# A decoder layer on one core: the first weight sums wait for the input's fetches, differences in place, five prepared weights moved into the mixer

## The chip, the cores and the metric

The kernel runs on one core of a Trainium2 chip. The time is device microseconds (us) of one execution; a kernel's time is the median of its runs. TensorE (PE) multiplies matrices, VectorE (DVE) and ScalarE (ACT) do element-wise work, GpSimd (POOL) does some of that and also issues transfers, and SyncE (SP) only issues transfers. Each engine takes its instructions in the order in which they stand in its own queue and waits at an instruction whose operands are not there.

## The reference

One layer: a SwiGLU feed-forward added at half weight, a mixer (stick-breaking attention beside a Mamba-2 scan), cross-attention on 256 memory tokens, and a second SwiGLU feed-forward, each between two RMS norms. The two feed-forwards are what the change touches most.

```python
D_MODEL, SEQ, D_FF = 1024, 1024, 2816

def swiglu(h, w_gu, w_down):
    gu = h @ w_gu
    g, u = jnp.split(gu, 2, axis=-1)
    return (jax.nn.silu(g) * u) @ w_down

    h = h + 0.5 * rmsnorm(swiglu(rmsnorm(h, ffn1_pre_g), ffn1_w_gu, ffn1_w_down), ffn1_post_g)
    h = h + rmsnorm(hybrid_mixer(rmsnorm(h, mix_pre_g), w_in, ...), mix_post_g)
    h = h + rmsnorm(memory_cross_attention(rmsnorm(h, xa_pre_g), rmsnorm(mem, mem_g), ...), xa_post_g)
    h = h + 0.5 * rmsnorm(swiglu(rmsnorm(h, ffn2_pre_g), ffn2_w_gu, ffn2_w_down), ffn2_post_g)
```

## The kernel before

**Every product in three.** An operand is split into a high part of fewer bits (cast on ScalarE) and the rest (subtracted on VectorE); `mm3` multiplies high by high, high by low and low by high. A weight tile of 128 x 1024 numbers or an input tile therefore costs a cast and a subtraction before TensorE can use it (`split`, lines 274 and 276).

**Seven products instead of eight.** The input stands transposed, as 8 tiles of 128 features for each of two halves of 512 tokens. Seen as a 2 x 2 matrix of blocks (B11 and B12: features 0 to 3 of half 0 and 1; B21 and B22: features 4 to 7), and gate and up weights as a 2 x 2 matrix too (G0, G1, U0, U1: their feature halves), a gate and an up column block need seven products of sums and differences. On the weights' side these sums are made on GpSimd for every block pair `f` (`pieces`: five of the seven blocks are sums, into a buffer `wc`, and then split). On the input's side they are made once for each feed-forward: S1 = B11 + B22, S4 = B11 + B12, S5 = B21 + B22, and in place B21 - B11 and B12 - B22, for `k` = 0 to 3. `seven(f)` runs the seven products: B22 and B21 into banks `a` and `b`, S1 into `c`, S4 into a fourth, and then B12 on top of `a`, S5 on top of `c` and B11 on top of `b`. Between them ScalarE copies `a` and `b` (lines 817 and 821), GpSimd takes their difference `d` (line 822), and VectorE makes `e = d + c` (line 827); the product with S5 may not write `c` before that `e` has read it. The first 3 block pairs of feed-forward 1 and the first 4 of feed-forward 2 are done plainly, with 24 matmuls for each gate or up block and half, while the sums are made.

**How the input's sums come about in feed-forward 1.** GpSimd issues the fetches: `fetch(k)` gets the four tiles of B11, B22, B12 and B21 for `k` (into `raw2`, two buffers, and `blk`), ("ca", k) gets B21 and B11 once more, and `again(k)` fetches B12 and B22 into the same buffers (`braw`; `rpost` and `dg`; `acc0` and `acc1`; `cb`). `steps(k)` are S1, S4 and S5, `below(k)` is B21 - B11, `differ(k)` the difference B12 - B22, and `last(k)` splits it. In feed-forward 2, `last(k)` scales B22, makes the difference in a buffer `wc` (three of them, shared with the weights' sums) and splits that.

**What sets the order.** TensorE's order is the program's. `self.clock` counts nominal nanoseconds of TensorE (216 for a matmul of 512 columns); `self.later` holds the side work with the clock from which it is written out, and `at(t, ...)` enters it there. Side work written out of `self.later` keeps the program's order on its engine (`kp`); the rest is placed by a scheduler by its priorities, so that an instruction can come to stand ahead of ones that the program writes earlier. The weights' sums are of the latter kind. `pinned` places the small matmuls of a norm at a clock.

**Prepared weights.** While feed-forward 1 runs, weights of the mixer are split ahead of time and put back to memory as high and low parts (`prepare`): for each half tile a fetch of 256 KB, a cast on ScalarE (line 212), a subtraction on VectorE (line 216) and two stores of 256 KB. `prepare_all` does this for 20 tiles of the scan's projection and the first `QKV` of the 24 tiles of q, k and v, at the clocks in `a`; transfers from clock 418000 on are issued by GpSimd, earlier ones by SyncE. The rest of the 24 are prepared in the scan (`ssd`), with SyncE issuing, which also issues the loads of the scan's own weights.

**Down-projection (`down7`).** Again seven products, over `m`, each of 11 row blocks; for `m` = 1, 2 and 3 TensorE goes on adding to the four banks of `m - 1`, once ScalarE (lines 1083, 1085, 1088) or VectorE has copied what stands there.

Of the kernel before, what the change touches and what calls it, by code (L numbers as in the profile page):

```python
# [14 lines left out]
ALU = mybir.AluOpType  # L15
# [10 lines left out]
MIXED = 6  # L26
QKV = 17
MEM = 256
# [19 lines left out]
class Kern:  # L48
# [200 lines left out]
    def prepare_all(self, sp):  # L249
        names = [("ssd", i) for i in [*range(6), *range(12, 26)]] + [("qkv", i) for i in range(QKV)]  # L250
        pairs = [
            ((self.fp, "acc0", None), (self.fp, "acc1", None)), ((self.fp, "rpost", None), (self.tp, "dg", None)),
            ((sp, "bh", None), (sp, "bl", None)),
        ]
        raw = [(sp, "braw", 2), (sp, "braw", 2), (self.xp, "xl0", KT + 1), (self.xp, "xl1", KT + 1)]
        n = 2 * len(names)
        a = [152000 + 4100 * i for i in range(n)]
        k = sum(t < 416000 for t in a)
        self.prepare(names, raw, pairs, a[:k] + [420000 + 12000 * i for i in range(n - k)], 418000)

# [308 lines left out]
    def up_phase(self, sp, sp2, wgu, gpre, act_d, bank, load, plain, sizes, rw=None, begin=None):  # L569
# [162 lines left out]
        def last(k):  # L732
            b, d = tmp["bd", k]
            if begin:
                self.split(*B12[k], b)
                return
            scale(d, k + 4)
            combine(B12[k], b, k, d, ALU.subtract)

# [12 lines left out]
        def pieces(f):  # L752
# [4 lines left out]
            for a, b, op in (  # L757
# [3 lines left out]
                if b is not None:  # L761
                    t = self.t(sp if begin else sp2, [P, 4, P], F32, "wc", bufs=NWC)
                    nc.gpsimd.tensor_tensor(out=t, in0=a, in1=b, op=op)  # L763
                    a = t
# [95 lines left out]
        Wb = blocks()  # L860
        t0, dt = (T0 + 12000, 7000) if begin else (T0 + 31000, 6500)
        early = [("ad", k) for k in range(4)] if begin else []
# [345 lines left out]
    def ssd(self, close):  # L1208

        nc, ap = self.nc, self.ap  # L1210
        with self.tc.tile_pool(name=self.nm("ssa"), bufs=1, reuse_waits="tile") as ep, \
# [344 lines left out]
            for i, ti in enumerate((8, 10, 0, 1)):  # L1556
                ps = self.proj_now(next(W), 1)
                if i == 0:
                    self.flush(1)
                    self.prepare(  # L1560
                        [("qkv", i) for i in range(QKV, 24)], *self.prep_pool(wsp),
                        [self.clock + 9000 + 8000 * i for i in range(2 * (24 - QKV))],
                    )
# [639 lines left out]
    def run(self):  # L2203
        nc, tc, ap = self.nc, self.tc, self.ap
        with tc.tile_pool(name="const", bufs=1) as cp, tc.tile_pool(name="state", bufs=1, reuse_waits="tile") as xp, \
# [54 lines left out]
            def begin(step):  # L2260
                if step < 0:
                    warm()
                elif step == 0:
                    load_x(0)
                elif step == 1:
                    consts()
                    norm_x(0, 8500, 13500)
                else:
                    load_x(1)
                    norm_x(1, 24000, 28000)  # L2270

# [112 lines left out]
```

## Time and profile before

| | |
|---|---|
| median of 3 runs | 2631.57 us (2626.02 to 2632.20) |
| the profiled execution's own time | 2630.33 us |
| its span, first to last instruction | 2628.6 us |
| TensorE busy | 2584.9 us, 98% of the span, 12850 matmuls |
| VectorE, ScalarE, GpSimd busy | 76%, 49%, 23% |
| memory traffic | 186 GB/s on average, 489.82 MB |

The profile is of one execution of the program. "Busy" is the time in which an engine runs at least one instruction; a matmul is counted as busy from its issue to its modelled end, so that matmuls overlap, and 98% does not mean that TensorE issues at its full rate all the time. A row of a timeline gives the start, the duration, the engine, the line of the kernel, the operation, what is written and read, and in brackets how long the engine was idle before it and what ended the wait. "PEclk" is the share of its full clock that TensorE was granted.

### The profile page before, as it was taken

To read this page: it belongs to the slowest core of one execution; us is meant where nothing else is said; L and a number is where in the kernel's file an instruction comes from. 1 tells how busy PE (TensorE), PEld (TensorE's weight loads), DVE (VectorE), ACT (ScalarE), POOL (GpSimd) and SP (SyncE) were. 2 spreads that over 40 slices of the span, in tenths; PEclk is the share of its full clock that TensorE was granted. 3 is DMA by queue.
4 is the path that set the end of the run, shared out by engine and by line. 5 is a ranking of instruction groups with operands and counts; after the bars stand their busy time and mean duration, and the time that the engine had idled before them with its cause. 6 is when DMAs were issued, how large, how long until landed. Compare 5 with 4: busy or idle time off the path is not lost. (4 is left out here: it accounts for less than half of the span.)

```text
span 2628.6 us, 36857 instructions
## 1 busy us (share of the span) xinstructions
PE 2584.9 (98%) x12850; PEld 2152.0 (82%) x12850; DVE 1988.5 (76%) x3044; ACT 1292.8 (49%) x2300; POOL 595.9 (23%) x708
## 2 busy tenths in 40 slices
PE   9899999999999999999999999999999999999999
PEld 7788888778777778888888897888878788888887
DVE  6878887779679775777777777767556888777767
ACT  7434444545356563555555555345554433333553
POOL 2555553110100001111111110101011655552000
PEclk9999999999999999999999999999999999999999
DMA  6458888875655226655555556547658453326654
GB/s 223 169 187 292 292 282 288 276 253 156 245 183 170 81 73 207 171 144 149 144 155 132 168 158 219 192 149 248 197 191 293 137 178 115 101 96 227 190 171 153
DMA packets 213546, 489.82 MB, mean 186 GB/s; under 512 B 26544, under 2 KB 35120, under 8 KB 213360
## 3 DMA queue, kind: packets, MB, share of 16 engines
q1 hardware_dynamic: 164192, 371.84, 43.8%
q0 software_dynamic: 25840, 73.16, 9.3%
q10 hardware_dynamic: 23328, 42.48, 4.3%
q8 instruction: 101, 1.65, 0.3%
q14 instruction: 85, 0.70, 0.1%
HBM read 327.46 MB, written 138.94 MB: 177 GB/s over the span
## 5 line engine op out<-in xcount | busy, mean ns | idle before, releaser
L139 PE MATMUL mm<-xh,whi 128*128 128x512 f32 x1320 | 520.2, 403 | 3.1 <-ACT xh L281 1.6
L139 PE MATMUL mm<-xl,whi 128*128 128x512 f32 (+1 forms) x1252 | 487.1, 389 | 2.2 <-DVE xl L276 1.7
L139 PE MATMUL mm<-xh,wlo 128*128 128x512 f32 x1272 | 488.5, 391 | 0.0
L139 PEld LDWEIGHTS mm<-xh,whi 128*128 128x128 f32 x1320 | 248.3, 188 | 44.7 <-issue 3.8
L139 PEld LDWEIGHTS mm<-xh,wlo 128*128 128x128 f32 x1272 | 238.8, 188 | 52.1 <-DVE wlo L276 0.4
L139 PEld LDWEIGHTS mm<-xl,whi 128*128 128x128 f32 x1252 | 236.1, 189 | 37.1 <-DVE xl L276 3.3
L1770 DVE TENSOR_TENSOR_SCAN nb<-nb,begin 128x128 f32<-128x128 f32 (+7 forms) x128 | 171.5, 1352 | 51.9 <-ACT nb L1766 51.0
L1766 ACT ACTIVATE nb<-z,scale 128x128 f32<-128x128 f32 (+2 forms) x192 | 107.9, 581 | 77.5 <-PE z L139 77.2
L276 DVE TENSOR_TENSOR wlo<-wraw,whi 128x1024 fp32r<-128x1024 f32 x70 | 85.5, 1221 | 54.1 <-ACT whi L274 50.7
L274 ACT CAST whi<-wraw 128x1024 fp32r<-128x1024 f32 (+1 forms) x87 | 83.8, 965 | 75.1 <-PE mm L139 52.3
L1787 POOL DMA_DIRECT2D mix<-sq x64 | 52.9, 826 | 229.8 <-DVE sq L1785 170.9
L670 ACT ACTIVATE ft<-ft 128x512 f32<-128x512 f32 x88 | 55.5, 632 | 99.2 <-DVE ft L669 98.5
L139 PE MATMUL dn<-xh,wlo 128*128 128x512 f32 x296 | 101.2, 390 | 1.3 <-DMA wlo<-dwlo 1.3
L763 POOL TENSOR_TENSOR wc<-wraw,raw 128x512 f32<-128x512 f32 x56 | 79.8, 1426 | 67.4 <-DVE whi L276 19.8
L763 POOL TENSOR_TENSOR wc<-raw,wraw 128x512 f32<-128x512 f32 x55 | 80.2, 1458 | 52.8 <-DVE wlo L276 21.8
L276 DVE TENSOR_TENSOR atl<-tr,ath 128x512 fp32r<-128x512 f32 (+1 forms) x108 | 67.9, 631 | 29.9 <-ACT ath L274 29.6
L848 POOL TENSOR_TENSOR ft<-ft,e 128x512 f32<-128x512 f32 x37 | 59.7, 1614 | 123.3 <-DVE e L847 47.6
L139 PE MATMUL mm<-ath,v 128*128 128x256 f32 x320 | 85.6, 290 | 0.5 <-ACT sq L1784 0.4
L274 ACT CAST ath<-tr 128x512 fp32r<-128x512 f32 (+1 forms) x108 | 58.9, 546 | 55.0 <-PE tr L142 50.7
L139 PE MATMUL dn<-xh,blk 128*128 128x512 f32 x264 | 85.1, 389 | 0.0
L274 ACT CAST whi<-wc 128x512 fp32r<-128x512 f32 x80 | 49.7, 621 | 68.7 <-PE dn L139 27.4
L139 PE MATMUL mm<-atl,v 128*128 128x256 f32 x320 | 82.7, 281 | 0.7 <-DVE atl L276 0.7
(584 smaller groups left out, 6801.6 us busy)
## 6 DMA issues: line engine op xcount, KB each, us to landing
whi<-dwhi SPq DMA_DIRECT2D x82, 512.0 KB, 3.7
wlo<-dwlo SPq DMA_DIRECT2D x82, 512.0 KB, 4.9
wraw<-in_w_gu SPq DMA_DIRECT2D x43, 512.0 KB, 4.2
raw<-in_w_gu SPq DMA_DIRECT2D x37, 512.0 KB, 4.2
dwhi<-bh SPq DMA_DIRECT2D x67, 256.0 KB, 4.3
dwlo<-bl SPq DMA_DIRECT2D x67, 256.0 KB, 4.3
wraw<-xs SPq DMA_DIRECT2D x56, 256.0 KB, 3.1
xs<-ft ACTq DMA_DIRECT2D x54, 256.0 KB, 3.1
```

The costliest lines, as they stand in the source:

```text
L139: self._pe(self.nc.tensor.matmul(out, lhsT, rhs, start=start, stop=stop, skip_group_check=self.more), cost)
L274: self.kp(self.nc.scalar.copy(hi, src))
L276: self.nc.vector.tensor_tensor(out=lo, in0=src, in1=hi.bitcast(F32), op=ALU.subtract)
L670: nc.scalar.activation(t, t, AF.Silu)
L763: nc.gpsimd.tensor_tensor(out=t, in0=a, in1=b, op=op)
L848: nc.gpsimd.tensor_tensor(out=t1, in0=t1, in1=e, op=ALU.mult)
L1766: nc.scalar.activation(nb[:, s0:s1], z[:, 0:n], AF.Sigmoid, scale=sc[:, i : i + 1])
L1770: nc.vector.tensor_tensor_scan(out=nb[:, 0:Wd][:, ::-1], data0=nb[:, 0:Wd][:, ::-1], data1=begin[:, S - Wd : S][:, ::-1], initial=0.0, op0 ...
L1787: nc.gpsimd.dma_start(out=self.mix_d[p][a * 64 : a * 64 + 64, csl], in_=o, accum_op=ALU.add)
```

## The change

Six edits. The weights' sums of the first block pair that goes through `seven` in feed-forward 1 now keep the program's order on GpSimd. `last` now scales B22 and makes the difference in place (`differ`) in feed-forward 2 too, and splits `b` in both; feed-forward 1 made it in place already, at an earlier clock, and does so still. `QKV` goes from 17 to 12: ten half tiles fewer in feed-forward 1 (64 in place of 74), ten more in the scan (24 in place of 14). The clocks in `a` begin 4000 earlier, stop at 388000 instead of 416000, and go on at 446000 in steps of 9000 instead of 420000 in steps of 12000: 59 and 5 half tiles, where it was 65 and 9. The step between the input's `k` in feed-forward 1 goes from 7000 to 6000, and that between half tiles in the scan from 8000 to 7000. The norm of the input's second half is pinned 2000 and 2500 earlier.

```diff
--- before.py
+++ after.py
@@ -24,7 +24,7 @@
 NFF = 22
 PLAIN = 3, 4
 MIXED = 6
-QKV = 17
+QKV = 12
 MEM = 256
 EPS = 1e-6
 
@@ -254,9 +254,9 @@
         ]
         raw = [(sp, "braw", 2), (sp, "braw", 2), (self.xp, "xl0", KT + 1), (self.xp, "xl1", KT + 1)]
         n = 2 * len(names)
-        a = [152000 + 4100 * i for i in range(n)]
-        k = sum(t < 416000 for t in a)
-        self.prepare(names, raw, pairs, a[:k] + [420000 + 12000 * i for i in range(n - k)], 418000)
+        a = [148000 + 4100 * i for i in range(n)]
+        k = sum(t < 388000 for t in a)
+        self.prepare(names, raw, pairs, a[:k] + [446000 + 9000 * i for i in range(n - k)], 418000)
 
     def wsrc(self, name, i):
         return self.ready[name, i] if (name, i) in self.ready else self.ap["w_" + name][i]
@@ -731,11 +731,10 @@
 
         def last(k):
             b, d = tmp["bd", k]
-            if begin:
-                self.split(*B12[k], b)
-                return
-            scale(d, k + 4)
-            combine(B12[k], b, k, d, ALU.subtract)
+            if not begin:
+                scale(d, k + 4)
+                differ(k)
+            self.split(*B12[k], b)
 
         def differ(k):
             b, d = tmp["bd", k]
@@ -760,7 +759,9 @@
             ):
                 if b is not None:
                     t = self.t(sp if begin else sp2, [P, 4, P], F32, "wc", bufs=NWC)
-                    nc.gpsimd.tensor_tensor(out=t, in0=a, in1=b, op=op)
+                    inst = nc.gpsimd.tensor_tensor(out=t, in0=a, in1=b, op=op)
+                    if begin and f == first_seven:
+                        self.tc.keep_in_program_order(inst)
                     a = t
                 n = self.nblk = (self.nblk + 1) % (6 + NBLK)
                 if n < 6:
@@ -858,7 +859,7 @@
 
         self.nblk = -1
         Wb = blocks()
-        t0, dt = (T0 + 12000, 7000) if begin else (T0 + 31000, 6500)
+        t0, dt = (T0 + 12000, 6000) if begin else (T0 + 31000, 6500)
         early = [("ad", k) for k in range(4)] if begin else []
         homes = {}
         if begin:
@@ -1559,7 +1560,7 @@
                     self.flush(1)
                     self.prepare(
                         [("qkv", i) for i in range(QKV, 24)], *self.prep_pool(wsp),
-                        [self.clock + 9000 + 8000 * i for i in range(2 * (24 - QKV))],
+                        [self.clock + 9000 + 7000 * i for i in range(2 * (24 - QKV))],
                     )
                     close()
                     sp = late.enter_context(self.tc.tile_pool(name=self.nm("ssb"), bufs=1, reuse_waits="tile", side="right"))
@@ -2267,7 +2268,7 @@
                     norm_x(0, 8500, 13500)
                 else:
                     load_x(1)
-                    norm_x(1, 24000, 28000)
+                    norm_x(1, 22000, 25500)
 
             self.kv_d = [[tc.dram_tile([P, 4, MEM], F32R, name=f"kv{h}{n}") for n in range(2)] for h in range(4)]
             self.h = [[ap["xT"][d, :, hh * H : (hh + 1) * H] for d in range(KT)] for hh in range(2)]
```

The order in which instructions stand moves at many places. Three are shown.

GpSimd near the beginning of feed-forward 1, before. Line 763 is the weights' sum and line 686 the input's fetches; `raw2` and `blk` belong to `fetch(k)`, the `braw`, `rpost`, `dg` to ("ca", k):

```order
L763 TENSOR_TENSOR wc_264_864<-wraw_261_854 128x512
L686 DMA raw2_146_542<-in_xT 128x512 x2
L686 DMA blk_147_545<-in_xT 128x512 x2
L686 DMA braw_232_674<-in_xT 128x512
L686 DMA braw_233_675<-in_xT 128x512
L686 DMA rpost_234_678<-in_xT 128x512
L686 DMA dg_235_679<-in_xT 128x512
L686 DMA raw2_236_692<-in_xT 128x512 x2
```

And with the change, further down the queue, where that sum (now line 762) stands:

```order
L686 DMA cb_243_796<-in_xT 128x512
L686 DMA braw_246_816<-in_xT 128x512
L686 DMA braw_247_817<-in_xT 128x512
L686 DMA rpost_249_836<-in_xT 128x512
L686 DMA dg_250_837<-in_xT 128x512
L762 ISA
L762 TENSOR_TENSOR wc_254_854<-wraw_251_844 128x512
```

The first sum moved from ahead of `fetch(2)` to behind the second fetch (`again`) of `k` = 0 and 1, and ("ca", 0) from ahead of `fetch(3)` to behind it.

VectorE in the first block pair of `seven` in feed-forward 1, before. The lines 276 are the low parts of weight blocks (`blk`, `whi`, `wlo` are places of weight tiles) and of B12 - B22 (`xl1`), line 827 is `e`:

```order
L276 TENSOR_TENSOR xl1_31_107<-cb_274_904,xh13_15_91 128x512
L276 TENSOR_TENSOR blk_293_1031<-wc_292_1029,blk_293_1031 128x512
L276 TENSOR_TENSOR blk_296_1051<-wraw_267_871,blk_296_1051 128x512
L276 TENSOR_TENSOR whi_299_1072<-wc_298_1070,whi_299_1072 128x512
L276 TENSOR_TENSOR wlo_302_1093<-wc_301_1091,wlo_302_1093 128x512
L827 TENSOR_TENSOR e_68_184<-sq1_282_962,dn_288_1005 128x512
```

With the change (line 884 multiplies the last plain gate block by its up block, line 742 is `differ`, line 828 is `e`):

```order
L742 SCALAR_TENSOR_TENSOR rpost_249_836<-rpost_249_836,params_3_78,dg_250_837 128x512
L884 TENSOR_TENSOR ft_259_866<-ft_259_866,mm_270_921 128x512
L276 TENSOR_TENSOR whi_255_856<-wc_254_854,whi_255_856 128x512
L276 TENSOR_TENSOR whi_267_913<-wc_266_911,whi_267_913 128x512
L276 TENSOR_TENSOR wlo_269_918<-wc_268_916,wlo_269_918 128x512
L742 SCALAR_TENSOR_TENSOR acc0_261_874<-acc0_261_874,params_3_78,acc1_262_875 128x512
L742 SCALAR_TENSOR_TENSOR cb_264_894<-cb_264_894,params_3_78,cb_265_895 128x512
L276 TENSOR_TENSOR whi_274_954<-wraw_251_844,whi_274_954 128x512
L276 TENSOR_TENSOR wlo_277_973<-wc_276_971,wlo_277_973 128x512
L276 TENSOR_TENSOR xl1_28_104<-braw_246_816,xh10_12_88 128x512
L828 TENSOR_TENSOR e_68_184<-sq1_272_952,dn_278_995 128x512
```

`e` moved from behind all four low parts of B12 - B22 and four of the next block pair to behind the first of the four; the low part of the very first weight block (`whi_255`) now stands behind two differences and behind line 884.

GpSimd in feed-forward 2, before, where the first block pair of `seven` (weights `wraw_4440`, `raw2_4441`) meets the second (`raw2_4465`, `wraw_4466`); line 822 is `d`:

```order
L763 TENSOR_TENSOR wc_4487_20492<-wraw_4440_20194,raw2_4441_20196 128x512
L763 TENSOR_TENSOR wc_4490_20511<-raw2_4441_20196 128x512
L822 TENSOR_TENSOR sq1_4471_20418<-sq1_4471_20418,sq0_4470_20417 128x512
L763 TENSOR_TENSOR wc_4492_20529<-raw2_4465_20381 128x512
L763 TENSOR_TENSOR wc_4499_20573<-raw2_4465_20381,wraw_4466_20383 128x512
```

With the change (line 823 is `d`):

```order
L762 TENSOR_TENSOR wc_4483_20488<-wraw_4440_20194,raw2_4441_20196 128x512
L762 TENSOR_TENSOR wc_4486_20507<-raw2_4441_20196 128x512
L762 TENSOR_TENSOR wc_4488_20525<-raw2_4465_20381 128x512
L762 TENSOR_TENSOR wc_4495_20569<-raw2_4465_20381,wraw_4466_20383 128x512
L762 TENSOR_TENSOR wc_4500_20592<-wraw_4466_20383,raw2_4465_20381 128x512
L762 TENSOR_TENSOR wc_4505_20630<-raw2_4465_20381,wraw_4466_20383 128x512
L823 TENSOR_TENSOR sq1_4471_20418<-sq1_4471_20418,sq0_4470_20417 128x512
```

`d` moved behind four sums of the next block pair.

## Prediction

> **What bounds the kernel now.** I read the page's table of busy time first, then the waits of TensorE alone, then windows of 30 us around the longest of them.
>
> ```profile
> PE 2584.9 (98%) x12850; PEld 2152.0 (82%) x12850; DVE 1988.5 (76%) x3044; ACT 1292.8 (49%) x2300; POOL 595.9 (23%) x708
> ```
>
> TensorE sets the time; the change removes none of its matmuls, so all that can be won is where it waits. The rows give who waits, for whom, the sum, how often, and the longest:
>
> ```profile
> PE dn L139 <- DVE e L827: 5.9, 2, 5.7
> PE mm L139 <- DVE e L827: 3.3, 2, 2.8
> PE dn L139 <- ACT F L1088: 3.1, 1, 3.1
> PE dn L139 <- ACT F L1083: 2.8, 1, 2.8
> PE mm L139 <- DVE xl L276: 1.7, 3, 0.7
> ```
>
> A wait also leaves TensorE slower behind it. These windows show busy time, and behind each "x" the matmuls issued; the last is undisturbed:
>
> ```profile
> 85.00:115.00 30.00, 22.60 (x86) 17.04 (x85) 25.54 (x30) 13.89 (x25) 20.15 (x16) 0.89 0.29 99
> 475.00:505.00 30.00, 27.15 (x114) 22.08 (x113) 22.37 (x37) 17.31 (x33) 3.21 (x6) 0.94 0.78 263
> 540.00:570.00 30.00, 26.86 (x112) 21.75 (x111) 21.16 (x35) 13.74 (x26) 2.15 (x4) 0.94 0.67 220
> 655.00:685.00 30.00, 28.32 (x124) 22.39 (x123) 22.00 (x38) 12.41 (x22) 5.35 (x10) 0.94 0.79 275
> 2085.00:2115.00 30.00, 27.17 (x114) 22.10 (x113) 26.68 (x30) 10.54 (x19) 19.84 (x17) 0.94 0.49 156
> 2125.00:2155.00 30.00, 30.00 (x135) 24.82 (x134) 24.94 (x30) 10.34 (x18) 19.89 (x17) 1.00 0.56 175
> ```
>
> Undisturbed, 135 matmuls go in 30 us. Before the changed places 49, 21, 23 and 21 are missing (first, second, third and fifth row). What one costs stands in the timeline of TensorE:
>
> ```profile
> 85.61 2.88 PE L139 MATMUL dn<-S,whi 128*128 128x512 f32 x12
> 88.33 2.88 PE L139 MATMUL dn<-S,wlo 128*128 128x512 f32 x12
> ...
> 102.37 5.10 PE L139 MATMUL dn<-S,wlo 128*128 128x512 f32 x12 [5.71 <-DVE e L827]
> ```
>
> Twelve start within 88.33 - 85.61 = 2.72 us, 0.227 each; behind the wait the same twelve take 5.10 where 2.88 is usual. So the places cost 11.1, 4.8, 5.2 and 4.8 us: 25.9 in all, 1% of the time, of which the waits are 16.1 (5.7 + 1.7 + 2.8 + 3.1 + 2.8) and the lower clock most of the rest. The Trainium skill (TensorE: Matmul & The Clock Gate, "Why this matters for your kernels") has the clock fall behind gaps over about 3 us; the granted clock of 0.94 around a 2.8 us wait shows a fall at a little less here. By the page the two waits of 2.8 us would be worth their bare length, and the sum below 2 to 4 us less.
>
> **The start of feed-forward 1 (11.1 us).** On GpSimd the first sum holds the queue:
>
> ```profile
> 46.94 1.29 POOL L763 TENSOR_TENSOR wc<-wraw 128x512 f32<-128x512 f32 x1 [30.32 <-DMA wraw<-in_w_gu]
> 50.83 1.09 POOL L686 DMA_DIRECT2D raw<-in_xT  x2 [2.60 <-issue]
> ...
> 59.27 1.06 POOL L686 DMA_DIRECT2D raw<-in_xT  x2 [4.18 <-issue]
> ```
>
> `fetch(2)` goes at 50.83, `fetch(3)` at 59.27, yet the sum alone costs them little: each also waits until VectorE has read the buffer's last user, which these two do:
>
> ```profile
> 49.54 0.74 DVE L702 SCALAR_TENSOR_TENSOR bl<-blk,params,raw 128x512 f32<-128x512 f32 x1
> ...
> 57.98 0.74 DVE L702 SCALAR_TENSOR_TENSOR bh<-blk,params,raw 128x512 f32<-128x512 f32 x1
> ```
>
> Those ends (50.28, 58.72) are what the norm's earlier pins and the shorter step move. The second half's norm comes 2500 of the clock earlier (2.6 us); I let the two reads follow by about 3 us, since on VectorE less stands ahead of them. So the fetches go near 47.5 and 55.5. The first sum and the second fetches come later in the queue than the fetches, and the price is the other end of this edit: the first sum is made not at 46.94 but behind `again(1)`, issued here so far:
>
> ```profile
> 77.24 0.56 POOL L686 DMA_DIRECT2D rpost<-in_xT  x1 [0.86 <-DVE bh L702]
> ...
> 95.28 1.73 POOL L822 TENSOR_TENSOR sq<-sq,sq 128x512 f32<-128x512 f32 x1
> ```
>
> 3 us earlier that is 74.2; two issues of 0.54 and 1.3 for the sum give 76.6. The first of the seven products starts 24 matmuls before 85.61, at 80.2; its third matmul needs the low part of this sum, which on VectorE stands behind the difference `rpost` (its tile lands and is scaled at 83.36 + 0.73 now, so near 80 or 81) and behind the gate times up product, which needs the matmul ending at 80.2. With 0.7 for each of the three and one stretched by a sum on GpSimd (1 more), it is done near 82.5 to 83: TensorE waits about 2.2 us where it did not wait.
>
> ```profile
> 83.36 0.73 ACT L689 ACTIVATE dg<-dg,params 128x512 f32<-128x512 f32 x1 [2.44 <-DMA dg<-in_xT]
> ```
>
> In return the old waits should go: `d` on GpSimd now stands ahead of the last sum of its block pair, where it stood behind that and two of the next pair, and `e` behind one low part of the difference instead of four and four of weights. If the seven products start at 82.4, `c` ends at 90.6, `e` follows by 92, and the product with S5 wants `c` at 96. So 11.1 - 2.2 = **8.9 us** won; 11.1 if the lost time is hidden, 2 to 4 if the first sum comes no earlier than `again(1)` does now.
>
> **The beginning of the down-projection (4.8 and 5.2 us).** Here ScalarE copies the banks late, behind splits that wait for transfers:
>
> ```profile
> 479.65 0.62 ACT L274 CAST hl<-wraw 128x512 fp32r<-128x512 f32 x1 [2.97 <-DMA wraw<-xs]
> ...
> 485.50 0.59 ACT L1083 ACTIVATE F<-dn 128x512 f32<-128x512 f32 x1
> ```
>
> Prepared halves share the stage: casts of line 212 on ScalarE, subtractions of line 216 on VectorE, with the share of the transfer engines in the last but one column.
>
> ```profile
> 430.00:488.00 58.00, 4.91 (x8) 0.98 0.91 325
> ```
> ```profile
> 430.00:488.00 58.00, 4.80 (x7) 0.98 0.91 325
> ```
>
> A matmul of 216 on the clock takes 0.227 us, so clocks 388000 and 446000 fall near 407 + 20 and 468 + 20 us, the 20 being the start and the first waits: between them the new table has nothing. Away go 8 halves x (4.91/8 + 4.80/7 = 0.61 + 0.69) us of the two engines and 8 x 0.77 MB, 6.1 MB, a third of 58 us x 325 GB/s = 18.9 MB. The copy is late by 2.8 us, behind a transfer that ended a wait of 2.97, so most of it should go; but the loads of the stage itself stay. I take two thirds, **3.2 us** (0 to 4.8). At 550 only the tail of the table is gone, and five halves come closer together (9000 for 12000): **2.2 us** (-1 to 5.2).
>
> **Feed-forward 2 (4.8 us).** Differences in place give back buffers `wc`, for one of which the fourth sum waited 7.08 us. What is late here, step by step on GpSimd:
>
> ```profile
> 2059.87 1.61 POOL L763 TENSOR_TENSOR wc<-wraw,raw 128x512 f32<-128x512 f32 x1 [7.08 <-DVE xl L276]
> ...
> 2086.41 1.62 POOL L848 TENSOR_TENSOR ft<-ft,e 128x512 f32<-128x512 f32 x1 [2.67 <-ACT blk L274]
> 2087.99 3.42 POOL L763 TENSOR_TENSOR wc<-raw 128x512 f32<-128x512 f32 x2
> 2091.38 1.71 POOL L822 TENSOR_TENSOR sq<-sq,sq 128x512 f32<-128x512 f32 x1
> ```
>
> The sums start 7 us earlier, so the splits that VectorE was behind with are done earlier; in the second block pair `d` then comes ahead of its need. The counterweight is the order: in the first block pair `d` now waits for four more sums. Side by side with a sum, a subtraction takes 1.78 instead of 0.69:
>
> ```profile
> 2072.72 1.78 DVE L276 TENSOR_TENSOR blk<-wc,blk 128x512 fp32r<-128x512 f32 x1
> ```
>
> Four such rounds are 7 us, as much as was won, so the first pair's S5 product waits for `e` some 1.4 us (0 to 3). Won: **3.4 us** (0 to 4.8).
>
> **The mixer.** Ten more halves between about 840 and 920 us: 10 x 0.69 on VectorE, 10 x 0.61 on ScalarE, 30 transfers.
>
> ```profile
> 840.00:920.00 80.00, 80.00 (x483) 63.66 (x483) 64.60 (x130) 45.55 (x75) 0.00 (x0) 1.00 0.26 93
> ```
>
> TensorE is fully covered there, VectorE has 15.4 us free for the 6.9, and transfers use 0.26: I charge **0.5 us** (0 to 4). In feed-forward 1 they are freed under a busy TensorE, worth nothing outside the stage above. The scaling, difference and split of `last` are as many instructions as before: nothing.
>
> **Sum.** 8.9 + 3.2 + 2.2 + 3.4 - 0.5 = 17.2 us off the profiled execution's 2630.3: 2613.1. The median before is 1.2 above that execution, so I say 2614.
>
> **Rivals.**
> The first sum is the new wait: if `again(1)` stays at 77.24, VectorE reaches the first block's low part near 87, TensorE waits 6.4 us and loses some 2.4 at the lower clock; of the first term 2.3 remain, 2620. For it: the buffers' reads, not the sum, hold the fetches. Against: the earlier norm. Chance 0.15.
> The stage's own loads keep the down-projection late: terms two and three vanish, 2619. For it: a share of 0.91, of which two thirds stay. Chance 0.14.
> Sums and subtractions block each other: the Trainium skill (SBUF — State Buffer, "SBUF: two separate sides") gives the pair of ports shared by VectorE and GpSimd to one instruction for its whole length; the 1.78 beside 0.69 agrees. As a mechanism here, with every round at 1.75 us, the six rounds ahead of `e` in feed-forward 2 put it 3 us late, with the lower clock 4.8: the fourth term is gone, 2617. Chance 0.12.
> The change does not do what it says: waits move but stay as long, gain below 5, 2627. Chance 0.08.
> Slower: in the scan a prepared half's stores stand in SyncE's queue ahead of the loads of the scan's weights, and wait for cast and subtraction. Held each by those and as much other work of VectorE and ScalarE, 2 x 1.3 us, the ten new halves delay the loads by 26 us together, and if nothing hides it that is 2613 + 26 = 2639. It decides once the loads held up exceed a tile's lead, which is the 48 matmuls of the tile before (10.9 us) less the landing:
> ```profile
> whi<-dwhi SPq DMA_DIRECT2D x82, 512.0 KB, 3.7
> ```
> Two or three halves in a row would have to be late at once; the full TensorE of the mixer's row speaks against it. Chance 0.10.
> The forecast has the rest, 0.41.
>
> **Range and chances.** All four places emptied gives 2630.3 - 25.9 = 2604. Towards the other side I reach to 2627: the cases with one term missing and the one that does nothing. Faster by over 0.3% (7.9 us, about what a measurement of this kernel can tell) means below 2623.7: forecast and the first three rivals, 0.82, less 0.07 for two of them together: 0.75. Within 0.3%: 0.15. Slower: 0.10.
>
> **What will show it.** Right: no `e` in the waits of TensorE near 95 us and 2090 us, 120 or more matmuls in the 30 us around the first products, `fetch(2)` before 49 us, and no line 212 between the start of the down-projection and the first copies. Wrong: TensorE waiting for `whi` at the first of the seven products for over 5 us, `e` again in feed-forward 2, loads `whi` landing late in the scan.

## The result, and the profile after

The changed kernel takes 2635.32 us (median of 12 runs, 2632.30 to 2639.01), the kernel before 2631.14 us in the same comparison (12 runs, 2626.02 to 2634.43): a ratio of 1.0019, with a 95% interval of 1.0010 to 1.0028. It is about 4 us (0.2%) slower: the interval lies above 1, but within the 0.3% that the prediction counts as no change. The prediction said 2614, and its range ended at 2627. The profiled execution has 2634.21 us and a span of 2632.4.

The page's busy times, and the longest rows of TensorE's waits (sum, times, longest):

```profile
PE 2586.2 (98%) x12850; PEld 2153.1 (82%) x12850; DVE 1990.6 (76%) x3044; ACT 1291.9 (49%) x2300; POOL 589.4 (22%) x696
```
```profile
PE dn L139 <- ACT F L1089: 9.1, 1, 9.1
PE mm L139 <- DVE e L828: 5.4, 2, 4.7
PE mm L139 <- DVE whi L276: 2.8, 1, 2.8
...
PE mm L139 <- ACT whi L274: 1.0, 1, 1.0
```

TensorE issues the same 12850 matmuls. Lines behind 763 have moved down by one: `e` is line 828, the copies into `F` (where the down-projection's results are collected) are 1084 and 1089; in the kernels below without the fixed place these numbers are two lower. Of the old list the 5.7 us for `e`, the 2.8 us for `F` near 486 and the wait in feed-forward 2 are gone. New are the waits for the first weight block (`whi`), another one for `e`, and a wait for `F` three times as long as any for `F` before. Windows of 30 us, in the columns used before (TensorE's matmuls behind the first "x", the granted clock third from the end):

```profile
85.00:115.00 30.00, 28.96 (x114) 23.11 (x115) 24.30 (x29) 13.12 (x23) 18.14 (x12) 0.91 0.22 79
105.00:135.00 30.00, 25.34 (x102) 20.45 (x101) 22.91 (x31) 9.85 (x18) 19.15 (x16) 0.89 0.49 167
475.00:505.00 30.00, 30.00 (x134) 24.84 (x133) 23.27 (x38) 18.81 (x35) 0.54 (x1) 1.00 0.64 208
540.00:570.00 30.00, 20.86 (x83) 16.74 (x82) 20.16 (x33) 10.30 (x19) 3.19 (x6) 0.83 0.69 230
2085.00:2115.00 30.00, 30.00 (x134) 24.82 (x134) 26.03 (x28) 10.35 (x19) 20.48 (x17) 1.00 0.37 122
```

Two of the four places are full now (134 matmuls). The window of the first products gained 28 matmuls, but the one at 105, which overlaps it, has 102, where it had 130. The window at 540 has 83, where it had 112.

Every trace has the same matmuls in the same order, but for some small ones of a norm near 40 us that the pins move. So the difference in the start of the same matmul says where time is won or lost. The table gives how much it grows in each stretch of the time before, for the profiled execution of each kernel (the experiments are told below) against the profiled execution before (us, minus is won; the last column is the last matmul's):

```
kernel                  start   ffn1 rest  ~486      ~550      scan      ffn2        whole
                        70-150  150-470    470-500   530-570   700-900   2070-2110
changed kernel            4.4     0.0       -4.5       6.6       0.2      -4.1         3.6
e1_resid_sync             4.7     0.0       -4.5       2.6       0.1      -4.1        -0.7
e2_old_halves             4.5     0.0       -0.9      -0.4      -0.1      -4.1        -1.2
e3_no_keep               -2.0     0.0       -4.5       5.6       0.2      -4.1        -5.3
e4_act_sums_later        -1.2     5.7       -4.5       5.6       0.2      -4.1         7.1
e5_no_tail                3.7     0.0       -4.5      -5.0       5.5      -4.1        -3.9
e6_keep_first             2.7     0.0       -4.5       5.9       0.2      -4.1         6.6
e7_no_keep_old_pins      -0.1     0.0       -4.5       5.3       0.1      -4.1        -3.5
e8_in_place              -0.5     0.0        0.7      -4.2       0.0      -4.1        -2.5
e9_combined              -2.4     0.2       -4.5      -5.0       0.3      -4.1       -11.3
e10_no_keep_resid_sync   -2.7     0.0       -4.5       1.1       0.2      -4.1        -7.3
e11_no_tail_gpsimd       -2.1     0.5       -4.5      -5.0       0.2      -4.1       -13.5
e12_table_alone           3.2     0.6       -4.3      -5.0       0.1      -4.1        -3.0
e13_no_keep_no_tail      -2.3     0.1       -4.5      -5.0       0.1      -4.1       -15.2
```

What is missing to the whole lies mostly between 900 and 2070 us, where no edit reaches and executions scatter from -1.3 to 5.5 us. So the whole of one execution says little, the single places a lot.

**The start.** At the first products, TensorE:

```profile
81.63 0.50 PE L139 MATMUL mm<-xh,whi 128*128 128x512 f32 x1 [1.00 <-ACT whi L274]
...
85.14 1.22 PE L139 MATMUL mm<-xh,whi 128*128 128x512 f32 x2 [2.77 <-DVE whi L276]
...
86.59 1.05 PE L139 MATMUL mm<-xh,whi 128*128 128x512 f32 x2
```

It waits 1.00 and 2.77 us, and three matmuls behind it take 86.59 - 85.14 = 1.45 us, twice the usual. The first wait is for ScalarE's cast of the first weight block, which stands behind the scaling of `dg`; the second is for the low part on VectorE (the last row), behind a stretched subtraction, two differences and line 884:

```profile
80.35 0.72 ACT L689 ACTIVATE dg<-dg,params 128x512 f32<-128x512 f32 x1 [0.17 <-DMA dg<-in_xT]
80.98 0.60 ACT L274 CAST whi<-wc 128x512 fp32r<-128x512 f32 x1
```
```profile
80.21 2.35 DVE L276 TENSOR_TENSOR xl<-bh,xh 128x512 fp32r<-128x512 f32 x1
82.48 0.74 DVE L742 SCALAR_TENSOR_TENSOR braw<-braw,params,braw 128x512 f32<-128x512 f32 x1
...
84.40 1.28 DVE L276 TENSOR_TENSOR whi<-wc,whi 128x512 fp32r<-128x512 f32 x2
```

On GpSimd, with the change:

```profile
47.69 1.06 POOL L686 DMA_DIRECT2D raw<-in_xT  x2 [31.25 <-DVE bl L702]
...
76.40 1.30 POOL L762 TENSOR_TENSOR wc<-wraw 128x512 f32<-128x512 f32 x1
...
93.55 1.29 POOL L823 TENSOR_TENSOR sq<-sq,sq 128x512 f32<-128x512 f32 x1 [5.50 <-ACT sq L822]
...
115.00 1.75 POOL L849 TENSOR_TENSOR ft<-ft,e 128x512 f32<-128x512 f32 x1
116.70 1.64 POOL L621 DMA_DIRECT2D cb<-act  x3
```

And before:

```profile
111.66 1.67 POOL L848 TENSOR_TENSOR ft<-ft,e 128x512 f32<-128x512 f32 x1 [1.00 <-DVE e L847]
113.28 1.64 POOL L621 DMA_DIRECT2D cb<-act  x3
```

The first sum is made at 76.40 instead of 46.94. `d` is 1.7 us earlier than before (93.55 for 95.28), and the old wait for `e` near 102 is gone; but the product of line 849 and the reads of `act` behind it come 3.3 and 3.4 us later. VectorE then meets two sums that need these reads ahead of the second pair's `e`:

```profile
124.26 1.29 DVE L628 TENSOR_TENSOR xl<-cb,cb 128x512 f32<-128x512 f32 x2 [3.30 <-DMA cb<-act]
125.47 0.68 DVE L828 TENSOR_TENSOR e<-sq,mm 128x512 f32<-128x512 f32 x1
```
```profile
126.20 2.08 PE L139 MATMUL mm<-S,wlo 128*128 128x512 f32 x4 [4.66 <-DVE e L828]
```

By the matmuls' starts, on the time before, 6.8 us are lost between 78 and 90, 9.3 won up to 110, and 6.9 lost again between 120 and 150: 4.4 lost.

**The down-projection near 557.** GpSimd, VectorE, ScalarE and TensorE, in this order:

```profile
543.61 0.54 POOL L226 DMA_DIRECT2D dwlo<-acc  x1 [3.62 <-DVE acc L216]
544.14 2.66 POOL L389 DMA_DIRECT2D xl<-in_xT  x5
```
```profile
553.77 0.69 DVE L1032 TENSOR_TENSOR cb<-raw,xl 128x512 f32<-128x512 f32 x1 [5.31 <-DMA raw<-in_w_dn]
...
555.58 0.68 DVE L1054 TENSOR_TENSOR ft<-dn,F 128x512 f32<-128x512 f32 x1
```
```profile
556.30 0.58 ACT L1089 COPY F<-dn 128x512 f32<-128x512 f32 x1 [9.60 <-DVE ft L1054]
```
```profile
556.94 1.65 PE L139 MATMUL dn<-hl,whi 128*128 128x512 f32 x3 [9.14 <-ACT F L1089]
558.38 1.05 PE L139 MATMUL dn<-hl,wlo 128*128 128x512 f32 x2
```

Read backwards: TensorE needs a bank that ScalarE copies; ScalarE's copy writes over a tile of `F` that VectorE must first have read (line 1054); VectorE has a sum or difference of weights ahead of that (line 1032), and that waits 5.31 us for a weight. While this weight is under way, GpSimd, free of prepared halves at 543.61, sends five reads of the residual at once (line 389, `resid`). Those belong to the stage behind, and before the change they went out behind the last half's stores:

```profile
581.19 3.71 POOL L389 DMA_DIRECT2D xl<-in_xT  x7
```

The two queues' shares of the transfer engines with the change (q0 is GpSimd's, q1 SyncE's), and the issues between 545 and 554 us, with the size and the median time to landing in us:

```profile
q0 software_dynamic: 480, 1.57, 53.5%
q1 hardware_dynamic: 730, 1.31, 39.7%
...
xl<-in_xT POOLq DMA_DIRECT2D x4, 256.0 KB, 6.5
raw<-in_w_dn SPq DMA_DIRECT2D x1, 256.0 KB, 7.0
```

The Trainium skill (DMA: Bandwidth & Descriptors, "Queues, rings and completion order") has each transfer engine take turns between the queues that have work. The two shares, near half each, fit that, though shares alone do not show the turns: the reads that nobody needed yet, with one store of the last half, took 53.5% of the engines, and the weight took 7.0 us to land, where such a load took 2.6 between 540 and 549 us of the profile before. How much of the wait the reads make is what e1 tests.

### The profile page after: what moved, and what is told of

Same layout as the page of the kernel before. It is cut to its first block, busy times and chain, and to the rows that moved or that the text cites. A ratio compares the mean times of both kernels' runs of the same rounds, so it can differ in the third digit from the quotient of the medians.

```text
span 2632.4 us, 36830 instructions
## 1 busy us (share of the span) xinstructions
PE 2586.2 (98%) x12850; PEld 2153.1 (82%) x12850; DVE 1990.6 (76%) x3044; ACT 1291.9 (49%) x2300; POOL 589.4 (22%) x696
## 4 chain that ended last, share of the span: by engine, by line
PE 86%; DVE 6%; DMA 2%; issue 2%; ACT 2%; POOL 0%; SPq 0%; DVEq 0%; ACTq 0%; POOLq 0%
PE mm L139 45%; PE dn L139 33%; PE z L139 2%; PE tr L142 2%; PE y L139 1%; PE ms L142 1%; PE ms L139 1%; PE seg L139 1%; DMA oraw<-mix 1%; DVE nb L1771 1%; DVE wlo L276 1%; DMA raw<-in_w_dn 1%; PE st L139 0%; DVE xl L276 0%; DVE whi L276 0%
## 5 line engine op out<-in xcount | busy, mean ns | idle before, releaser
L1767 ACT ACTIVATE nb<-z,scale 128x128 f32<-128x128 f32 (+2 forms) x192 | 107.8, 580 | 77.7 <-PE z L139 77.5
L762 POOL TENSOR_TENSOR wc<-wraw,raw 128x512 f32<-128x512 f32 x56 | 79.4, 1418 | 51.0 <-DVE whi L276 15.9
L849 POOL TENSOR_TENSOR ft<-ft,e 128x512 f32<-128x512 f32 x37 | 59.8, 1616 | 121.4 <-DVE e L848 53.5
L139 PE MATMUL dn<-hl,whi 128*128 128x512 f32 x288 | 76.0, 397 | 9.1 <-ACT F L1089 9.1
L274 ACT CAST wlo<-wc 128x512 fp32r<-128x512 f32 x79 | 49.1, 621 | 71.3 <-PE dn L139 21.9
```

The costliest lines, as they stand in the source:

```text
L139: self._pe(self.nc.tensor.matmul(out, lhsT, rhs, start=start, stop=stop, skip_group_check=self.more), cost)
L274: self.kp(self.nc.scalar.copy(hi, src))
L762: inst = nc.gpsimd.tensor_tensor(out=t, in0=a, in1=b, op=op)
L849: nc.gpsimd.tensor_tensor(out=t1, in0=t1, in1=e, op=ALU.mult)
L1767: nc.scalar.activation(nb[:, s0:s1], z[:, 0:n], AF.Sigmoid, scale=sc[:, i : i + 1])
```

## The experiments

**e1_resid_sync**: the residual's reads in SyncE's queue, behind the loads.

```diff
-            self.kp(self.nc.gpsimd.dma_start(out=self.XL[hh][d], in_=self.h[hh][d]))
+            self.kp((eng or self.nc.gpsimd).dma_start(out=self.XL[hh][d], in_=self.h[hh][d]))
...
-                self.resid(0, 3500, 16000)
+                self.resid(0, 3500, 16000, self.nc.sync)
```

> The changed kernel with one edit: in the first down-projection the eight reads of the residual (line 389) are issued on SyncE behind the weight loads that stand ahead of them, not on GpSimd, where the changed kernel sends five of them at 544.14 to 546.26 us. Theory (the five reads at once fill the transfers, the load that a subtraction of line 1032 needs lands after 7.0 us, and the copy F of line 1089 stands behind that subtraction): the wait of 9.1 us near 557 falls below 3 us, and the span by 6 us or more against the changed kernel's 2632.4. Rival (the five prepared halves, 9000 apart on the clock where they were 12000 apart, are themselves too much for this place): the wait stays at 6 to 9 us.

```profile
PE dn L139 <- ACT F L1089: 4.6, 1, 4.6
```

The wait halves, from 9.1 to 4.6, and 4.0 us are won at the place. The reads are about half of the cause; with 4.6 us left and 4.3 off the span, the theory expected too much.

**e2_old_halves**: `QKV`, the table `a` and the scan's step as before, all else changed.

```diff
-QKV = 12
+QKV = 17
...
-        a = [148000 + 4100 * i for i in range(n)]
-        k = sum(t < 388000 for t in a)
-        self.prepare(names, raw, pairs, a[:k] + [446000 + 9000 * i for i in range(n - k)], 418000)
+        a = [152000 + 4100 * i for i in range(n)]
+        k = sum(t < 416000 for t in a)
+        self.prepare(names, raw, pairs, a[:k] + [420000 + 12000 * i for i in range(n - k)], 418000)
```

> The changed kernel with the old preparation: 17 qkv weights in feed-forward 1 at the old times, seven in the scan at the old step; the sums' order, the pins, the step of the fetches and the differences in place stay as changed. Theory (the table alone made both differences in the down-projection): near 486 the wait for F of line 1084 is back with about 2.8 us, near 550 it is 3 us and not 9, and the start of feed-forward 1 (waits near 81, 85 and 126 us) and feed-forward 2 (no wait near 2093) are as in the changed kernel. Rival (the down-projection comes 4.65 us later in the changed kernel, and that shift alone moved its transfers): the wait near 550 stays above 6 us, or none comes near 486.

```profile
PE dn L139 <- ACT F L1084: 3.0, 2, 2.8
PE dn L139 <- ACT F L1089: 2.7, 1, 2.7
```

Both as the theory has it, though TensorE arrives 5 us later than before: the table made both differences, not the shift. Near 486 the wait is as long as before (2.80 us, before 2.85); the 0.9 us that this kernel keeps there is the clock, which stayed at 1.00 behind it.

**e3_no_keep**: the sums without their fixed place.

```diff
-                    inst = nc.gpsimd.tensor_tensor(out=t, in0=a, in1=b, op=op)
-                    if begin and f == first_seven:
-                        self.tc.keep_in_program_order(inst)
+                    nc.gpsimd.tensor_tensor(out=t, in0=a, in1=b, op=op)
```

> The changed kernel without the fixed place of the first block pair's sums on GpSimd; pins and step as changed. Theory (with the order kept, GpSimd idles 5.50 us for the subtraction that stands ahead of the last three sums, all later splits slip, and the first sum's split stands behind the scaling of the second refetch): the waits near 81 and 85 us go, the wait for e near 126 falls from 4.7 to below 2 us, and the start as a whole (first products to 150 us) is at least 4.65 us shorter than in the changed kernel, so no longer than before. Rival (the first sum goes ahead of the third fetch again and holds it, as before): waits near 95 to 102 us of 5 us or more for e come back, and the start is as long as before or longer.

```profile
47.15 1.29 POOL L762 TENSOR_TENSOR wc<-wraw 128x512 f32<-128x512 f32 x1 [31.25 <-DMA wraw<-in_w_gu]
48.38 1.09 POOL L686 DMA_DIRECT2D raw<-in_xT  x2
```
```profile
PE dn L139 <- DVE e L826: 4.5, 2, 3.8
PE mm L139 <- DVE e L826: 1.6, 2, 1.1
```

The start is 6.4 us shorter than in the changed kernel and 2.0 shorter than before. The sum goes ahead of the fetch again, and that costs the fetch 0.69 us (48.38 for 47.69). For this the fixed place had put the first sum off by 29 us. A wait for `e` (here line 826) comes back, with 3.8 instead of 5.7 us: the rival was half right on that, not on the length. The start repeats from kernel to kernel: without the fixed place it wins 2.0 to 2.7 us in five (e3, e9, e10, e11, e13); with the place as in the change, and no other edit there, it loses 3.2 to 4.7 in five (the changed kernel, e1, e2, e5, e12).

**e4_act_sums_later**: the sums of activations with block pairs 6 and 7.

```diff
-            if later_sums and (f in (4, 5) if begin else f > 6 and f % 2):
+            if later_sums and (f in (6, 7) if begin else f > 6 and f % 2):
```

> The changed kernel, with the two groups of activation sums (lines 621 and 628) taken with the block pairs 6 and 7 of feed-forward 1 and not with 4 and 5. Theory (VectorE's queue has two of these sums, waiting for transfers that GpSimd issued late, ahead of e at 125.47): the wait for e near 126 us falls from 4.7 to below 1.5 us, and 3 to 6 us are won there with the clock. Rival (e is late because GpSimd's own subtraction, at 120.37, stands behind late sums): the wait stays above 2 us.

```profile
185.14 2.11 PE L139 MATMUL dn<-S,blk 128*128 128x512 f32 x8 [3.46 <-DVE e L828]
```

At the `e` near 126 TensorE waits 1.3 instead of 4.7 us, as the theory has it, so 3.4 were the sums that wait for reads ahead of it; in the rest VectorE waits for GpSimd's late `d` (1.17 us ahead of this `e`). The work only moves: 5.7 us are lost later in the stage, with the wait of 3.46 above.

**e6_keep_first**: the fixed place for the first sum alone.

```diff
-                    if begin and f == first_seven:
+                    if begin and f == first_seven and self.nblk < 0:
```

> The changed kernel, with the fixed place on GpSimd for the first sum alone; the only instructions that change places there are the fifth sum and the subtraction of line 823 of the first block pair. Theory (two separate costs: the first sum's late place makes the waits near 81 and 85 us, 7.07 us of the start; the subtraction ahead of later sums makes the wait near 126): the waits near 81 and 85 stay at 3 to 4.5 us together, and the wait near 126 falls below 2 us. Rival (both come from the late first sum): near 126 the wait stays at 4 us or more.

```profile
124.88 2.58 PE L139 MATMUL mm<-S,wlo 128*128 128x512 f32 x6 [4.63 <-DVE e L828]
```

The waits near 81 and 85 stay (1.42 and 2.35 us), as expected, but near 126 the rival holds: with `d` behind the fifth sum the wait is the same. The late first sum is enough. Its delay runs through the chain of sums and splits: the product of line 849 comes at 113.68 here, at 109.79 in e3_no_keep.

**e7_no_keep_old_pins**: as e3_no_keep, with the norm's pins and the step of before.

```diff
-        t0, dt = (T0 + 12000, 6000) if begin else (T0 + 31000, 6500)
+        t0, dt = (T0 + 12000, 7000) if begin else (T0 + 31000, 6500)
...
-                    norm_x(1, 22000, 25500)
+                    norm_x(1, 24000, 28000)
```

> The changed kernel without the fixed place of the sums, with the old pins (24000, 28000) and the old step of 7000: of the start, everything as before the change; the preparation and the differences in place stay as changed. Theory (pins and step alone are a gain, as e3_no_keep is 1.72 us ahead of before at 150 us): the start is as before, within 0.6 us at 150 us, so e3_no_keep's pins and step are worth 1 to 2.3 us. Rival (the norm's timing does nothing, the start of e3_no_keep is luck of transfers): this one is also 1 us or more ahead of before at 150 us. The wait near 550 to 557 is 8 us or more in both cases.

The start is as before (-0.1, with the 5.7 us for `e`), and the wait near 550 is 8.4 us: pins and step together are worth the 2 us of e3_no_keep.

**e8_in_place**: the kernel before, with the differences in place alone.

```diff
-            if begin:
-                self.split(*B12[k], b)
-                return
-            scale(d, k + 4)
-            combine(B12[k], b, k, d, ALU.subtract)
+            if not begin:
+                scale(d, k + 4)
+                differ(k)
+            self.split(*B12[k], b)
```

> The kernel before with the differences in place alone. Theory (the buffers wc that they give back, and nothing else, made the wait for e near 2093 go): no wait near 2093, 4 to 5 us less from there on, everything ahead of 1990 us as before within 1 us. Rival (the wait went since the changed kernel reaches feed-forward 2 some 7 us later against its transfers): the wait of 4.8 us with the clock stays in part, 2 us or more.

```profile
2053.96 1.31 POOL L762 TENSOR_TENSOR wc<-wraw,raw 128x512 f32<-128x512 f32 x1
```

Feed-forward 2 gives the same 4.1 us as in the changed kernel, and TensorE waits for nothing there: the differences in place do it alone. The row is the sum that waited 7.08 us for a buffer before; here it waits for none, so the buffers given back are what moved. The place near 550 was 4.2 us better with nothing changed there (a wait of 0.5 us, where the profile before had 3.1): with the old table its wait differs between executions, so its first 3 us are no fixed cost. With the new table, its five late halves and the reads on GpSimd it was 7.6 to 9.1 in five kernels.

**e5_no_tail**: e1_resid_sync, and no halves behind 446000; six more go to the scan.

```diff
-QKV = 12
+QKV = 9
...
-        self.prepare(names, raw, pairs, a[:k] + [446000 + 9000 * i for i in range(n - k)], 418000)
+        self.prepare(names, raw, pairs, a[:k], 418000)
...
-                        [self.clock + 9000 + 7000 * i for i in range(2 * (24 - QKV))],
+                        [self.clock + 9000 + 5600 * i for i in range(2 * (24 - QKV))],
```

> The changed kernel with the residual's reads on SyncE as in e1_resid_sync, and without the five halves that stand behind 446000: nine qkv weights are prepared in feed-forward 1, all before the down-projection, and fifteen in the scan, at a step of 5600 for 7000. Theory (the five halves make what e1_resid_sync left of the wait near 552, 4.6 us): the wait falls below 2 us, about 3 us or more are won against e1_resid_sync there, and the six halves more in the scan cost below 1 us, since the ten that the change itself moved there cost nothing that can be seen. Rival (the weights and sums that the down-projection itself loads keep the copies late): 3 to 4.6 us stay. Third: the scan's queue now holds up its weights, and the scan (700 to 900 us) grows by 2 us or more.

TensorE's waits from 690 to 910 us:

```profile
PE st L139 <- DVE xdec L1387: 1.8, 2, 1.6
PE seg L139 <- ACT L L1357: 1.4, 2, 0.7
...
```

The theory holds for the down-projection: no wait is left at 550, 5.0 us better than before. The scan loses 5.5, as in the third case, but not by its way: TensorE waits there for VectorE and ScalarE, not for the scan's weights. Ten more halves had cost the scan 0.2; six more, and the shorter step with them, cost 5.5. Which of the two does it was not separated.

**e9_combined, e11_no_tail_gpsimd, e10_no_keep_resid_sync**: parts put together. Without a tail, all 64 halves stand ahead of the down-projection at a shorter step.

```diff
-        a = [148000 + 4100 * i for i in range(n)]
+        a = [148000 + 3700 * i for i in range(n)]
...
-        self.prepare(names, raw, pairs, a[:k] + [446000 + 9000 * i for i in range(n - k)], 418000)
+        self.prepare(names, raw, pairs, a[:k], 418000)
```

> A version meant to keep what each part won: the changed kernel without the fixed place of the sums (e3_no_keep), with the residual's reads on SyncE (e1_resid_sync), and with all 64 prepared halves ahead of the down-projection, 3700 apart for 4100, so that none stands behind 446000 and the scan prepares no more than in the changed kernel. Theory (the costs found are separate and add up): the start 2 us ahead of before, the place near 486 4.5, the place near 550 5, feed-forward 2 4.3, together 13 to 16 us less than before: 2615 to 2619. Rival (halves at 3700 are too many for feed-forward 1, as thirty were for the scan): TensorE waits between 150 and 400 us, where it waits for nothing in any kernel so far, and 5 us or more of that are lost.

> e9_combined with the residual's reads back on GpSimd, where nothing stands ahead of them now. Theory (the burst of these reads delays the loads of the down-projection whatever stands ahead of it): they are issued as their buffers come free, and the wait near 550 is 2 us or more longer than in e9_combined. Rival (the burst hurt only together with the five halves' stores): no difference above 1 us.

> The changed kernel without the fixed place of the sums and with the residual's reads on SyncE; the five halves behind 446000 stay. Theory (the gains add): start 2 us and the place near 486 4.5 us ahead of before, the place near 550 as before or 1.5 us worse, feed-forward 2 4.3 us ahead: 9 to 11 us less than before. Rival (where TensorE arrives 6 us earlier at the place near 550 its loads are as late as they were, and the gain is given back there): under 6 us less than before.

e9_combined takes 2621.65 us (5 runs), a ratio of 0.9964 to the kernel before (0.9951 to 0.9976); e10 takes 2622.76 (8 runs), 0.9967 (0.9957 to 0.9978). At the four places e9 won 16.0 us, as expected, and feed-forward 1 bears the shorter step (0.2). The median is 3 us above the expected 2619; 3.8 us went between 900 and 2070. e10, with the five halves, still waits 4.2 us near 545, and its median is 8.6 us below that of before, just short of the expected 9 to 11. e11 tells of the reads. With no halves ahead of them five go out at once, 89 us earlier than in the changed kernel, and the other three from 560.96 on:

```profile
455.03 2.71 POOL L389 DMA_DIRECT2D xl<-in_xT  x5
560.96 0.54 POOL L389 DMA_DIRECT2D xl<-in_xT  x1 [103.22 <-issue]
```

TensorE waits for nothing between 430 and 600 us, and the place is as empty as in e9. So the same burst does no harm at 455. The expectation's question is left open by this: what five reads at 544 would cost without the halves is not shown, since they are not there at that time.

**e12_table_alone**: the changed kernel with that table and nothing else.

> The changed kernel with one edit, the table: all 64 prepared halves ahead of the down-projection, 3700 apart, none behind 446000; the sums keep their fixed place and the residual's reads stay on GpSimd. Theory (the five halves are the one cause of the wait near 557, directly by their stores and by what they do to the buffers that the residual's reads take): the wait of 9.1 us is below 1 us, the start stays 4 to 5 us behind before, and the median is 9 to 12 us below the changed kernel's: 2623 to 2627. Rival (with the late start TensorE meets the transfers of the stage at another moment, and a wait of 3 us or more stays without the halves): 2628 or more.

```profile
540.00:570.00 30.00, 30.00 (x134) 24.86 (x133) 22.41 (x36) 14.60 (x27) 1.07 (x2) 1.00 0.58 188
```

2624.98 us (10 runs), 0.9985 of the kernel before (0.9976 to 0.9995), and the place is full. The two lines of the table take 9 us off the changed kernel by the two ratios (1.0019 - 0.9985, of 2631), and 11.6 at the place: the five late halves are the cause of the whole wait, directly and by way of the reads, five of which go out at 459.94 here. The step of 3700 is not what empties the place: in e5, with 4100, it is as empty. The start loses 3.2, a little less than expected.

**e13_no_keep_no_tail**: e11_no_tail_gpsimd, timed.

> e11_no_tail_gpsimd again, timed: no fixed place of the sums, 64 halves ahead of the down-projection at 3700, the residual's reads on GpSimd. Theory (the four places give 2, 4.5, 4.5 and 4.3 us): 2614 to 2619, 0.5 to 0.6% below before. Rival (its one profile met a favourable moment in the mixer, where e9_combined had 2 to 5 us more in transfers): 2620 or more, as e9_combined.

```profile
85.00:115.00 30.00, 25.45 (x98) 19.98 (x97) 23.52 (x27) 14.25 (x26) 22.01 (x18) 0.89 0.33 116
```

2615.48 us (5 runs, 2615.38 to 2618.96), 0.9955 of the kernel before (0.9941 to 0.9970), as the theory has it: 0.45% below the kernel before, and 16.8 us below the changed one by the two ratios. Three of the four places are full, with 134 matmuls each; of the start, the row above, 2.3 of 11.1 us are won. The median of e9 is 6 us higher, but the two were timed in different comparisons: by their ratios they are 2.4 us apart, and the intervals overlap, so no difference between them is shown.

## Why the prediction was wrong

- **What bounds the kernel** was right: four places, 25.9 us, the waits and the clock behind them. e13 wins 15.9 us at them; the forecast for the change was 17.7.
- **The start, 8.9 won: 4.4 lost.** This is the first step that failed. Up to the first sum its working held: `fetch(2)` went at 47.69 (47.5 expected), and the sum was done at 77.7 (76.6). But the prediction itself said that the buffers' reads hold the fetches and "the sum alone costs them little" (0.69 us by e3), so the fixed place had little to win. Its price was put at one wait of 2.2 us, at its bare length, though the same text had counted the lower clock behind every other wait: it was 1.00 + 2.77 us, and 6.8 with the clock. Left out were ScalarE's cast, which stands behind the scaling of `dg`, and what stood on VectorE ahead of the difference `rpost`: a subtraction stretched to 2.35 us and another difference. And the step asked what becomes of the old wait, not what is late next: the product of line 849 came 3.3 us later than before, so TensorE, 2.2 us early by then, paid 6.9 us at the next pair. Of the signs named for the start two came true, no `e` near 95 and `fetch(2)` before 49 us, and the start still lost; the third did not (114 matmuls in the window, not 120). The rival that the first sum is the new wait came nearest, though `again(1)` did come earlier (75.24); it too ended at the first products.
- **Near 486, 3.2 won: 4.5 won.** The mechanism was right (e2, with the old halves, has the wait back), and the term too small: TensorE waits there no more.
- **Near 550, 2.2 won (-1 to 5.2): 6.6 lost.** This is the second step that failed. It priced the five halves by the work that they add and not by what stands behind them in GpSimd's queue. The old tail had held the residual's reads back to 581 us; with a shorter one they went out at 544, among the stage's loads. e1 shows 4.0 us for the reads, e12 11.6 for the halves and what they bring about. The 5.2 us to be won were read from one execution, too: in e8 the old table cost 4.2 us less.
- **Feed-forward 2, 3.4 won: 4.1 won**, by the differences in place and the buffers that they give back (e8). The mechanism was right; the delay of 1.4 us in the first pair did not come.
- **The mixer, 0.5 lost: 0.2.** SyncE's queue, the slower rival, did not show with ten more halves. With sixteen more the scan did lose 5.5 us, by another way: VectorE and ScalarE.

The terms as measured (a loss has the minus) are -4.4 + 4.5 - 6.6 + 4.1 - 0.2 = -2.6 us; the spans differ by 3.8, and the other 1.2 are parts of 0.5 us or less in other stretches.

## What to carry to other kernels

When an instruction's place is fixed or a queue gets shorter, list what stood behind it, on that engine and in its transfers, and when each would now go out: work held back by accident is released, too, and may go out when it does harm (five reads at 544 us) or when it does none (the same five at 455). Where side engines are as far behind as TensorE is ahead, a wait that goes comes back at the next point where TensorE needs them; count the stage, not the wait. And price a new wait as the old ones are priced, with the clock behind it.

## What the runs showed of the hardware

The price of the lower clock does not grow with the wait. Behind the 2.77 us (85.14 to 86.59 in the rows above) and behind the 9.14 us (556.94 to 558.38) three matmuls take 1.45 and 1.44 us, twice the usual, and 12 and 10 matmuls go at that rate. Behind the waits of 3.8 to 9.1 us in feed-forward 1 and its down-projection, over all profiles, it was 6 to 14 matmuls, which costs 1.4 to 2.9 us over the twenty matmuls behind each: 1.7 behind 8.41 us in e7, 2.8 behind 4.59 us in e1.

Whether the clock falls is not settled by the length of the wait alone. These are the three us behind a lone wait of 2.85 us in the kernel before (at 486.15) and behind the wait of 3.46 us in e4 (at 185.14), with the matmuls behind the first "x" and the granted clock third from the end:

```profile
486.00:489.00 3.00, 2.85 (x7) 2.27 (x8) 3.00 (x6) 2.73 (x7) 1.61 (x3) 0.50 0.65 187
```
```profile
185.00:188.00 3.00, 2.86 (x12) 2.36 (x13) 3.00 (x6) 0.62 (x1) 0.62 (x1) 1.00 0.71 231
```

The Trainium skill (TensorE: Matmul & The Clock Gate, "Why this matters for your kernels") puts the fall behind gaps of over about 3 us. Here 2.85 us did it and 3.46 us did not, and the measurement decides. An estimate from these figures: where the clock falls behind each, three waits of 3 us cost 3 to 6 us more than one of 9, since each fall costs 1.4 to 2.9.
